# Zero-padded 128-row weights for RWKV's two low-rank products, and one buffer instead of three for its exponentials

## The chip, the cores and the metric

The kernel runs on one core of a Trainium2 chip. The metric is the time of one execution on the device in microseconds (us). The engines named below are PE (TensorE, matrix products), DVE (VectorE), ACT (ScalarE), POOL (GpSimd) and SP (SyncE, which here issues DMAs only). Each works through its own queue of instructions in order, and waits for the others by semaphores.

## The reference

One step of a single hybrid decoder layer: 1024 prompt tokens of a new sequence and 8 sample tokens that continue stored states, width 1024. A normalised input goes through one combined projection, whose columns feed three recurrences (RWKV-7, HGRN2, RG-LRU); their outputs go through an output projection, and then an MLP of width 4096 follows.

```python
xn = _rmsnorm(x, prm['norm1_g'][l])
P = (xn @ w_in).astype(F32)
pr, ph, pl = jnp.split(P, [RWKV_COLS, RWKV_COLS + HGRN_COLS], axis=-1)
pm = pr + prm['mu_shift'][l] * (pr_prev - pr)
...
mix = jnp.concatenate([o_r, o_h, o_l], axis=-1).astype(dt)
x = x + mix @ prm['w_out'][l]
xn2 = _rmsnorm(x, prm['norm2_g'][l])
x = x + jnp.square(jax.nn.relu(xn2 @ prm['mlp_w1'][l])) @ prm['mlp_w2'][l]
```

The change touches RWKV-7 alone. Of its columns `xw` and `xa` are 64 wide each; from them come the decay and the learning rate, by two low-rank products:

```python
r, k, v, xw, xa, xg = jnp.split(pm, [c, 2 * c, 3 * c, 3 * c + W_LORA, 3 * c + W_LORA + A_LORA], axis=-1)
w_log = -jax.nn.softplus(-(w0 + jnp.tanh(xw) @ w_up)) - 0.5
decay = jnp.exp(-jnp.exp(w_log))
a = jax.nn.sigmoid(a0 + xa @ a_up)
g = jax.nn.sigmoid(xg) @ g_up
...
S = S * wt[:, :, None, :] + sa[..., None] * (kkt * at)[:, :, None, :] + vt[..., None] * kt[:, :, None, :]
```

## The kernel before, in words

Channels lie on the 128 partitions and tokens along the free dimension. The large products (projections `in`, output projection `out`, MLP `up` and `dn`) take three passes each: weights and activations are split into a high and a low part (`wh`, `wl`, `xh`, `xl`, the type fp32r), and the kernel adds xh·wh, xl·wh and xh·wl (`dense_steps`). The small products of the recurrences are plain fp32, and one of them shows in the trace as two matmuls of the same shape. All products are recorded at one line (L74, the helper `mm`) and all transposes at L78, so that the trace tells them apart by the names of their tiles.

The program has two stages. Stage 1 projects and runs the recurrences; its tokens go in two halves of 512 (`hf` 0 and 1; the 8 sample tokens are with the second). RWKV's six heads are three blocks `j` of 128 channels, and each half has two quarters `qt` of 256 tokens, so that there are 12 parts `q` = (j, hf, qt). A part passes through `rw_operands` (operands from the projected columns), `rw_inverse` (the inverse within chunks of 64 tokens), `rw_chain` (four chunks after another with the state) and `rw_finish` (group norm, gate). Stage 2 is the MLP.

In stage 1 generators for all these are woven into one program (`weave`): each yields after a piece of work and names a delay or an event that it waits for, and the planner takes the next one that is due by its own estimate of PE time; the projections fill what is left. **PE's order is that of the code so written.** The order on DVE, ACT and POOL is set by the list scheduler behind the language, from priorities and modelled durations. So an edit can move instructions on those three queues far from the edited line, while PE's rows stay.

What the change touches:

- `waup` [128, 384] is one tile with two weights: rows 0 to 63 hold w_up, rows 64 to 127 a_up. The tile `xwa` (in the trace `pm_wa`) has tanh(xw) in rows 0 to 63 and xa in rows 64 to 127. The product `pw` (decay) uses rows 0 to 63 of both, `pa` (learning rate) rows 64 to 127; each is made once in a part, and each waits in ACT's tanh (L513, L522). `rw_sample_lora` makes the same products for the 8 sample tokens (`s_lora`).
- `ee` [128, 4, 65] is the exponential of the cumulated decay of a part, with a 1.0 ahead of each chunk (written by POOL's memset, L533). `ar` (two DVE operations, the first at L550) reads all of it. Later `rw_chain` reads the last column of each chunk as `wc`, to scale the state (POOL `ws` L691, DVE `st` L697). Thus it has three buffers.
- `hst` holds states of HGRN2 per chunk, in ten buffers.

Other names that the trace shows at these places: `t` is scratch of a part; `ir_kk` (L245 on DVE, then a power on POOL at L129) and `t` (L248), transposed by PE as `pb_kk`, form the norm of the key; `s_…` are the sample tokens' operands (L775 to L807); `ot` (L728) is the normalised output of a part, which PE transposes as `oT`; `gs` its group-norm sums; `rh` (L670) the right-hand side of a chunk, which PE multiplies into `ch`; `hf`, `lf`, `b` and `kq` belong to HGRN2 (L855 to L932); `xsq` is the square for the first norm.

Of the kernel before, what the change touches and what calls it, by code (L numbers as in the profile page):

```python
# [9 lines left out]
F32 = mybir.dt.float32  # L10
# [7 lines left out]
P = 128  # L18
# [9 lines left out]
QT = 256  # L28
NQ = QT // 64
C = 64  # L30
# [21 lines left out]
def kernel(ctx: ExitStack, tc: tile.TileContext, i, o):  # L52
# [169 lines left out]
    nsp2 = const.tile([P, 2], F32, name="nsp2")  # L222
    V.tensor_scalar(nsp2, sp2, -2.0, None, op0=ALU.mult)

    waup = const.tile([P, 384], F32, name="waup")
    gup = const.tile([P, 384], F32, name="gup")


# [262 lines left out]
    def rw_operands(q):  # L491

        j, hf, qt = PARTS[q]
        n = f"{j}_{hf}_{qt}"
        q0 = qt * QT
        qs = slice(q0, q0 + QT)
        jc = slice(j * P, (j + 1) * P)
        yield ("lora", hf)
        yield ("rkv", j, hf)
        xwa, _ = lora[hf]  # L500
        r, k, v = rkv[j, hf]

        def ck(ap):
            return ap.rearrange("p (c t) -> p c t", t=C)

        r_, k_, v_ = r[:, qs], k[:, qs], v[:, qs]
        t1, t2, t3, t4, t5 = (w2(f"t{u}", n, 1) for u in range(1, 6))

        act(t2, k_, AF.Square, scale=vec("kk", j))

        pw = ps("o", f"pw_{n}")
        mm(pw[:, 0:QT], waup[0:64, jc], xwa[0:64, qs])
        act(t1, pw[:, 0:QT], AF.Tanh, bias=hw0[:, j:j + 1], scale=0.5)  # L513
        V.tensor_scalar(t1, t1, -DECAY, -DECAY, op0=ALU.mult, op1=ALU.add)
        yield D4
        pn = yield from head_inv_root(t2, QT, f"kk{n}", "o", 1e-24, t4)
        V.scalar_tensor_tensor(t4, k_, vec("kk", j), pn, op0=ALU.mult, op1=ALU.mult)
        V.tensor_tensor_scan(t2, rmask_f, t1, 0.0, op0=ALU.mult, op1=ALU.add)
        yield D5
        pa = ps("o", f"pa_{n}")  # L520
        mm(pa[:, 0:QT], waup[64:128, jc], xwa[64:128, qs])
        act(t3, pa[:, 0:QT], AF.Tanh, bias=ha0[:, j:j + 1], scale=0.5)  # L522
        if q >= 3:
            yield ("C", q - 3)
        if q >= 1:
            yield ("sc", q - 1)
        yield D6
        ee = rwp.tile([P, NQ, C + 1], F32, tag="ee", name=f"ee_{n}", bufs=3)
        ar = rwp.tile([P, NQ, 2, C], F32, tag="ar", name=f"ar_{n}", bufs=3)
        kb = rwp.tile([P, NQ // 2, 4, C], F32, tag="kb", name=f"kb_{n}", bufs=1)  # L530
        kbt = rwp.tile([P, NQ, P], F32, tag="kbt", name=f"kbt_{n}", bufs=3)
        uv = rwp.tile([P, NQ, P], F32, tag="uv", name=f"uv_{n}", bufs=3)
        G.memset(ee[:, :, 0:1], 1.0)  # L533
        act(ee[:, :, 1:C + 1], ck(t2), AF.Exp)
        act(t1, t2, AF.Exp, scale=-1.0)

        pt = ps("o", f"vT_{n}")
        for c in range(NQ // 2):
            tr(pt[:, c * P:(c + 1) * P], v[:, q0 + c * P:q0 + (c + 1) * P], ident)
        pt4 = pt[:, 0:NQ // 2 * P].rearrange("p (c x) -> p c x", x=P)  # L540
        S.copy(uv[0:64, 0:NQ:2, :], pt4[0:64])
        S.copy(uv[64:128, 1:NQ:2, :], pt4[64:128])
        ck4 = "p (c x t) -> p c x t"
        V.scalar_tensor_tensor(t5, t3, 1.0, t4, op0=ALU.add, op1=ALU.mult)
        V.scalar_tensor_tensor(kb[:, :, 1:3, :], t5.rearrange(ck4, x=2, t=C), 0.5, t1.rearrange(ck4, x=2, t=C),
                               op0=ALU.mult, op1=ALU.mult)
        V.tensor_scalar(t3, t3, hka[:, j:j + 1], omka[:, j:j + 1], op0=ALU.mult, op1=ALU.add)
        V.tensor_tensor(t3, t3, k_, op=ALU.mult)
        V.tensor_tensor(kb[:, :, 0:4:3, :], t3.rearrange(ck4, x=2, t=C), t1.rearrange(ck4, x=2, t=C), op=ALU.mult)
        V.scalar_tensor_tensor(ar[:, :, 0, :], ck(t4), -1.0, ee[:, :, 0:C], op0=ALU.mult, op1=ALU.mult)  # L550
        V.tensor_tensor(ar[:, :, 1, :], ck(r_), ee[:, :, 1:C + 1], op=ALU.mult)
        ev(("A", q), L_OPS)
        V.scalar_tensor_tensor(t5, r_, vec("rk", j), t3, op0=ALU.mult, op1=ALU.mult)
        yield D7

        pt = ps("o", f"kbt_{n}")
        for c in range(NQ):
            src = kb[:, c // 2, 2 * (c % 2):2 * (c % 2) + 2, :].rearrange("p x t -> p (x t)")
            tr(pt[:, c * P:(c + 1) * P], src, ident)
        S.copy(kbt, pt.rearrange("p (c x) -> p c x", x=P))  # L560
        if q >= 2:
            yield ("P", q - 2)
        yield D8
        bo = w2("bo", n)
        pb = ps("o", f"bonus_{n}")[:, 0:QT]
        mm(pb, bones, t5)
        V.tensor_tensor(bo, pb, v_, op=ALU.mult)
        if qt == 1:
            free["pm"] += 3
        live[q] = dict(ee=ee, ar=ar, kb=kb, kbt=kbt, uv=uv, bo=bo)  # L570
        ev(("A2", q), L_EV)
        yield D9

# [78 lines left out]
    def rw_chain(q):  # L652
# [1 line left out]
        j, hf, qt = PARTS[q]  # L654
        n = f"{j}_{hf}_{qt}"
        yield ("B", q)
        ee, ar, kbt, uv, sc, ym, xm = (live[q][x] for x in ("ee", "ar", "kbt", "uv", "sc", "ym", "xm"))
        pt = ps("ch", f"ch_{n}")
        po = pt[:, QT:2 * QT]
        for c in range(NQ):  # L660
            st = rw_state[j]
            b = brow[c % 2]
            first = st is None
            mv = xm[b, (c // 2) * 2:(c // 2) * 2 + 2, :].rearrange("p h v -> p (h v)")
            if first:
                rh = mv
            else:
                mm(pt[b, 0:P], ar[:, c, 0, :], st)
                rht = rwp.tile([P, P], F32, tag="rh", name=f"rh{c}_{n}", bufs=1)
                V.tensor_tensor(rht[b, :], pt[b, 0:P], mv, op=ALU.add)  # L670
                rh = rht[b, :]
                yield D16
            for h in range(2):
                hc = slice(h * 64, h * 64 + 64)
                mm(pt[b, hc], ym[b, (c // 2) * 2 + h, :], rh[:, hc])
            V.tensor_copy(uv[b, c, :], pt[b, 0:P])
            yield D17
            for h in range(2):
                hp = slice(h * 64, h * 64 + 64)
                mm(pt[hp, P:P + 64], kbt[:, c, hp], uv[:, c, hp])  # L680
            out = po[krow[c % 2], (c // 2) * P:(c // 2) * P + P]
            if not first:
                mm(out, ar[:, c, 1, :], st, stop=False)
            for h in range(2):
                hp = slice(h * 64, h * 64 + 64)
                mm(out[:, hp], sc[:, 2 * c + h, 64:128], uv[:, c, hp], start=first, stop=first or h == 1)
            wc = ee[:, c, C:C + 1]
            sn = rw_st[j][c % 2]
            if not first:
                ws = rwp.tile([P, P], F32, tag="ws", name=f"ws{c}_{n}", bufs=2)  # L690
                G.tensor_scalar(ws, st, wc, 0.0, op0=ALU.mult, op1=ALU.add)  # L691
            for h in range(2):
                hp = slice(h * 64, h * 64 + 64)
                if first:
                    V.tensor_scalar(sn[hp, hp], pt[hp, P:P + 64], wc[hp], None, op0=ALU.mult)
                else:
                    V.scalar_tensor_tensor(sn[hp, hp], pt[hp, P:P + 64], wc[hp], ws[hp, hp], op0=ALU.mult, op1=ALU.add)  # L697
            rw_state[j] = sn
            if c == NQ - 1:

                if q >= 1:
                    yield ("N", q - 1)
                ot = w2("ot", n, 1)
                sums = small.tile([P, 2, NQ], F32, tag="gs", name=f"gs_{n}", bufs=2)
                for g in range(NQ):
                    act(ot[:, g * 64:(g + 1) * 64], po[:, g * 64:(g + 1) * 64], AF.Copy, accum_out=sums[:, 0, g:g + 1])
                live[q].update(ot=ot, sums=sums)
                ev(("C", q), 0.5)
            yield D18
# [33 lines left out]
    def rw_sample_lora():  # L743
        tcol = slice(HT, HW)
        xwa, sg = lora[1]
        out = hgp.tile([P, 3, 3, NB], F32, name="s_lora")
        for q, (w, x) in enumerate(((waup[0:64], xwa[0:64]), (waup[64:128], xwa[64:128]), (gup, sg))):
            pl = ps("h", f"s_lora{q}")
            for j in range(3):
                mm(pl[:, j * NB:(j + 1) * NB], w[:, j * P:(j + 1) * P], x[:, tcol])  # L750
# [151 lines left out]
    def hg_half(j, hf, lf, kin, q, iv, gs):  # L902
# [101 lines left out]
        for c in range(NCK):  # L1004
            st = hg_state[j]
            pc = ad[:, c % 2, (c // 2) * C:(c // 2 + 1) * C]
            sn = pool.tile([P, C], F32, tag="hst", name=f"hst{c}_{n}", bufs=10)
            if st is None:
                V.tensor_copy(sn, pc)
            else:  # L1010
# [271 lines left out]
    def projections():  # L1282
# [3 lines left out]
        for hf in range(2):  # L1286
            for group, j in ORDER[hf]:
                yield from dict(w=rw_lora, r=rw_proj, h=hg_proj, l=lru_proj)[group](j, hf)
                if (group, hf) == ("w", 0):
                    x_load(1, place=tc.keep_in_program_order)  # L1290
                    ev(("x", 1), 8.0)
                    for dst, name in ((cmask, "masks"), (waup, "waup"), (gup, "gup"), (cst, "lcst")):
                        nc.sync.dma_start(dst, i[name])
                    for h in range(2):
                        nc.sync.dma_start(lruw[h * 64:h * 64 + 64, :, h * 64:h * 64 + 64], i["lruw"][h])
            if hf == 0:
# [255 lines left out]
```

## Time and profile before

| | before |
|---|---|
| time, median of 3 runs (lowest, highest) | 1618.23 us (1614.12, 1618.76) |
| the profiled execution's own time | 1615.32 us |
| its span in the trace | 1613.5 us |
| granted PE clock, mean over the span | 0.967 |
| PE busy | 1534.4 us, 95% of the span, 12158 matmuls |
| DVE busy | 775.8 us, 48% |
| ACT busy | 637.1 us, 39% |
| POOL busy | 376.9 us, 23% |
| DMA, mean share of 16 queues' time: software queue, hardware queue | 26.3%, 15.3% |
| read from HBM | 144.12 MB |

"Busy" is the time in which an engine had an instruction in execution. PE's matmuls are pipelined, so their durations overlap: what a matmul costs PE is read from the distance between the starts of its neighbours, not from its own duration. "Granted clock" is the share of full speed at which PE was let run. In a list of instructions in order of time a row gives start, duration, engine, line, operation, tiles, shapes and a count; a bracket at its end gives how long the engine had stood idle before it, and what released it. In a table by stretches a row gives the stretch, its length, the busy time of PE, PE's weight loads, DVE, ACT and POOL with counts, then the granted clock, the share of DMA and the GB/s.

### The profile page before, as it was taken

The numbers are of one execution on the slowest core, as the hardware profiler recorded it, in microseconds if no ns is written. First come the engines' busy times: TensorE is split into PE (matmuls) and PEld (weight loads), VectorE is DVE, ScalarE is ACT, GpSimd is POOL, SyncE is SP. The second block draws the span as 40 slices with busy tenths as digits, with TensorE's granted clock in tenths as the row PEclk, the third lists the DMA queues.
The fourth block names the chain that finished last, engine by engine and source line by source line (L and its number), as shares of the span: only waits on it lengthen the run. The fifth ranks groups of instructions, "written<-read, shape, count | busy, mean of one in ns | idle before, by whom it ended". The sixth has DMA issues, their size and how long they took to land. (4 is left out here: it accounts for less than half of the span.)

```text
span 1613.5 us, 29358 instructions
## 1 busy us (share of the span) xinstructions
PE 1534.4 (95%) x12158; PEld 1310.5 (81%) x12158; DVE 775.8 (48%) x1765; ACT 637.1 (39%) x1361; POOL 376.9 (23%) x492
## 2 busy tenths in 40 slices
PE   8879899999899999899987999999999999999997
PEld 6657677688788788777787889989898989899887
DVE  7476656775656676675465222222232222222224
ACT  4444633653445355355344323233232423233232
POOL 4462312322323423423222010111101010111111
PEclk8979989999799999999999999999999999999999
DMA  6524424333243434434433353545445353544342
GB/s 216 134 53 95 90 67 92 80 80 86 60 91 75 100 80 101 99 81 113 113 119 103 82 109 80 108 85 104 83 101 92 79 110 81 104 85 89 58 90 106
DMA packets 54501, 152.18 MB, mean 94 GB/s; under 512 B 7104, under 2 KB 7392, under 8 KB 54368
## 3 DMA queue, kind: packets, MB, share of 16 engines
q0 software_dynamic: 24416, 70.67, 26.3%
q1 hardware_dynamic: 29808, 79.61, 15.3%
q8 instruction: 95, 1.56, 0.4%
q14 instruction: 38, 0.31, 0.1%
q10 hardware_dynamic: 144, 0.04, 0.0%
HBM read 144.12 MB, written 6.17 MB: 93 GB/s over the span
## 5 line engine op out<-in xcount | busy, mean ns | idle before, releaser
L74 PE MATMUL in<-xh,wl_in 128*128 128x512 f32 (+3 forms) x648 | 226.3, 349 | 6.5 <-DMA wl_in<-in_w_in 6.5
L74 PE MATMUL in<-xl,wh_in 128*128 128x512 f32 (+3 forms) x648 | 224.4, 346 | 3.4 <-DVE xl L357 3.4
L74 PE MATMUL in<-xh,wh_in 128*128 128x512 f32 (+3 forms) x648 | 225.4, 348 | 0.0
L74 PE MATMUL dn<-hh,wl_w 128*128 128x264 f32 (+2 forms) x696 | 223.3, 321 | 0.2 <-DMA wl_w<-in_w 0.2
L74 PE MATMUL dn<-hh,wh_w 128*128 128x264 f32 (+2 forms) x696 | 223.0, 320 | 0.0
L74 PE MATMUL dn<-hl,wh_w 128*128 128x264 f32 (+2 forms) x696 | 223.0, 320 | 0.0
L1440 DVE TENSOR_TENSOR mix<-mix,dn 128x512 f32<-128x512 f32 (+2 forms) x192 | 98.4, 512 | 241.6 <-PE dn L74 241.6
L268 POOL DMA_DIRECT2D wl_w<-in_w x88 | 76.3, 874 | 577.3 <-ACT hh L1370 323.6
L263 ACT ACTIVATE wh_w<-raw_w 128x512 fp32r<-128x512 f32 (+1 forms) x90 | 70.6, 784 | 272.5 <-PE dn L74 224.5
L1369 DVE SCALAR_TENSOR_TENSOR rl<-up,rl 128x512 f32<-128x512 f32 (+2 forms) x96 | 49.6, 516 | 222.3 <-ACT rl L1368 222.3
L74 PE MATMUL up<-nxh,wh_w 128*128 128x264 f32 (+1 forms) x512 | 145.7, 285 | 1.5 <-DVE rl L1369 1.3
L74 PEld LDWEIGHTS in<-xh,wl_in 128*128 128x128 f32 x648 | 128.2, 198 | 22.5 <-DMA wl_in<-in_w_in 8.0
L74 PE MATMUL up<-nxl,wh_w 128*128 128x264 f32 (+1 forms) x512 | 145.0, 283 | 0.5 <-POOL nxl L1268 0.5
L74 PE MATMUL up<-nxh,wl_w 128*128 128x264 f32 (+1 forms) x512 | 145.2, 284 | 0.0
L74 PEld LDWEIGHTS dn<-hh,wl_w 128*128 128x128 f32 x696 | 131.0, 188 | 13.8 <-DMA wl_w<-in_w 3.8
L74 PEld LDWEIGHTS in<-xl,wh_in 128*128 128x128 f32 x648 | 127.8, 197 | 17.5 <-DVE xl L357 4.3
L74 PEld LDWEIGHTS in<-xh,wh_in 128*128 128x128 f32 x648 | 128.6, 198 | 15.8 <-issue 4.7
L74 PEld LDWEIGHTS dn<-hl,wh_w 128*128 128x128 f32 x696 | 131.1, 188 | 10.0
L74 PEld LDWEIGHTS dn<-hh,wh_w 128*128 128x128 f32 x696 | 131.2, 188 | 9.2
L74 PE MATMUL up<-nh,wl_w 128*128 128x512 f32 x256 | 102.7, 401 | 5.9 <-DMA wl_w<-in_w 5.9
L1368 ACT ACTIVATE rl<-up 128x512 f32<-128x512 f32 (+2 forms) x96 | 43.3, 451 | 152.4 <-PE up L74 152.4
L74 PE MATMUL up<-nh,wh_w 128*128 128x512 f32 x256 | 102.6, 401 | 0.0
(438 smaller groups left out, 3215.8 us busy)
## 6 DMA issues: line engine op xcount, KB each, us to landing
raw_in<-in_w_in SPq DMA_DIRECT2D x53, 512.0 KB, 3.4
wl_in<-in_w_in POOLq DMA_DIRECT2D x49, 512.0 KB, 5.6
raw_w<-in_w SPq DMA_DIRECT2D x32, 512.0 KB, 3.3
raw_w<-in_w SPq DMA_DIRECT2D x64, 256.0 KB, 2.7
wl_w<-in_w POOLq DMA_DIRECT2D x30, 512.0 KB, 5.4
wl_w<-in_w POOLq DMA_DIRECT2D x58, 256.0 KB, 4.1
raw_out<-in_w_out SPq DMA_DIRECT2D x16, 512.0 KB, 3.4
wl_out<-in_w_out POOLq DMA_DIRECT2D x8, 512.0 KB, 5.6
```

What stands on the lines that cost most here:

```text
L74: PE.matmul(out, lhsT, rhs, start=start, stop=stop)
L263: act(wh[:, ks], raw[:, ks], AF.Copy)
L268: G.dma_start(wl[:, ks], src[:, ks], accum_op=ALU.add)
L1368: act(rl[:, :n], pt[:, :n], AF.Relu)
L1369: V.scalar_tensor_tensor(rl[:, :n], pt[:, :n], 0.0, rl[:, :n], op0=ALU.max, op1=ALU.mult)
L1440: V.tensor_tensor(x2[m][:, c0:c0 + n], x2[m][:, c0:c0 + n], pt[:, :n], op=ALU.add)
```

## The change

Two weight tiles of 128 rows take the place of `waup`: `wup` has w_up in rows 0 to 63 and zeros below, `aup` zeros above and a_up in rows 64 to 127. The products `pw`, `pa` and `s_lora` then run over all 128 rows of `xwa`; the zeros cancel the other half. `ee` keeps one buffer: its last columns are copied into a small tile `wc` [128, 4] with three buffers, which `rw_chain` reads instead. `hst` has nine buffers.

```diff
-    waup = const.tile([P, 384], F32, name="waup")
+    wup, aup = (const.tile([P, 384], F32, name=nm) for nm in ("wup", "aup"))
+    G.memset(wup[64:128], 0.0)
+    G.memset(aup[0:64], 0.0)
...
-        mm(pw[:, 0:QT], waup[0:64, jc], xwa[0:64, qs])
+        mm(pw[:, 0:QT], wup[:, jc], xwa[:, qs])
...
-        mm(pa[:, 0:QT], waup[64:128, jc], xwa[64:128, qs])
+        mm(pa[:, 0:QT], aup[:, jc], xwa[:, qs])
...
-        ee = rwp.tile([P, NQ, C + 1], F32, tag="ee", name=f"ee_{n}", bufs=3)
+        ee = rwp.tile([P, NQ, C + 1], F32, tag="ee", name=f"ee_{n}", bufs=1)
+        wc = rwp.tile([P, NQ], F32, tag="wc", name=f"wc_{n}", bufs=3)
...
         act(t1, t2, AF.Exp, scale=-1.0)
+        V.tensor_copy(wc, ee[:, :, C])
...
-            wc = ee[:, c, C:C + 1]
+            wc = wcs[:, c:c + 1]
...
-        for q, (w, x) in enumerate(((waup[0:64], xwa[0:64]), (waup[64:128], xwa[64:128]), (gup, sg))):
+        for q, (w, x) in enumerate(((wup, xwa), (aup, xwa), (gup, sg))):
...
-            sn = pool.tile([P, C], F32, tag="hst", name=f"hst{c}_{n}", bufs=10)
+            sn = pool.tile([P, C], F32, tag="hst", name=f"hst{c}_{n}", bufs=9)
...
-                    for dst, name in ((cmask, "masks"), (waup, "waup"), (gup, "gup"), (cst, "lcst")):
+                    for dst, name in ((cmask, "masks"), (gup, "gup"), (cst, "lcst")):
                         nc.sync.dma_start(dst, i[name])
+                    for h, w in enumerate((wup, aup)):
+                        hp = slice(h * 64, h * 64 + 64)
+                        nc.sync.dma_start(w[hp], i["waup"][hp])
```

On PE every row stands where it stood, with other weights in 24 + 6 products. SP has one load more, ahead of `lruw`. POOL has two memsets more at the start. DVE has 12 copies more, one in each part ahead of the first `ar`. Line numbers after the weight tiles are 3 to 8 higher in the changed kernel. Beyond that the scheduler has moved rows on DVE and POOL, and the following places are those that matter for what is said below.

The first is DVE's queue around 410 to 419 us, where the sixth part (j, hf, qt = 2, 0, 1) is in its chain (`rh`), the output of the fifth is normalised (`ot`), and the samples of RWKV's first block (`s_…`) and HGRN2's second half (`b`, `kq`) are prepared. Before, the four `ot` stood four rows above this piece:

```order
L910 SCALAR_TENSOR_TENSOR b_1_4680<-rmask,lf_1_4674 128x256 x2
L924 TENSOR_TENSOR kq_0_1_4693<-b_1_4680 128x512
L924 TENSOR_TENSOR kq_0_1_4802<-b_1_4680 128x512
L786 SCALAR_TENSOR_TENSOR s_kk_4159<-s_kk_4159,s_q_4160 128x8
L802 TENSOR_TENSOR s_tm_4149<-s_st_4148,s_kk_4159 128x512
L787 SCALAR_TENSOR_TENSOR s_ka_4162<-s_kk_4159,s_a_4153 128x8
L788 TENSOR_SCALAR s_q_4160<-s_a_4153,vt 128x8
L789 SCALAR_TENSOR_TENSOR s_kn_4161<-s_q_4160,sm_k 128x8
L790 SCALAR_TENSOR_TENSOR s_bo_4163<-sm_r,vt,s_kn_4161 128x8
L775 TENSOR_SCALAR s_a_5774<-s_a_5774 128x8
L670 TENSOR_TENSOR rh_2_0_1_4242<-ch_0_1_4240,xm_0_1_3492 64x128
```

The same place of the changed kernel on DVE:

```order
L791 SCALAR_TENSOR_TENSOR s_kk_4177<-s_kk_4177,s_q_4178 128x8
L807 TENSOR_TENSOR s_tm_4167<-s_st_4166,s_kk_4177 128x512
L792 SCALAR_TENSOR_TENSOR s_ka_4180<-s_kk_4177,s_a_4171 128x8
L793 TENSOR_SCALAR s_q_4178<-s_a_4171,vt 128x8
L675 TENSOR_TENSOR rh_2_0_1_4260<-ch_0_1_4258,xm_0_1_3508 64x128
L915 SCALAR_TENSOR_TENSOR b_1_4700<-rmask,lf_1_4694 128x256 x2
L794 SCALAR_TENSOR_TENSOR s_kn_4179<-s_q_4178,sm_k 128x8
L780 TENSOR_SCALAR s_a_5796<-s_a_5796 128x8
L733 TENSOR_SCALAR ot_0_0_4107<-ot_0_0_4107,gs_0_0_4108 128x64 x4
L929 TENSOR_TENSOR kq_0_1_4713<-b_1_4700 128x512
L929 TENSOR_TENSOR kq_0_1_4822<-b_1_4700 128x512
```

`rh` now stands ahead of `b` and both `kq`, and the four `ot` behind `rh` and `b`.

The second is POOL's queue at the same time (`gs` and `s_q` are the powers that the group norm and the samples wait for, `wl_in` the issue of a weight load). Before:

```order
L129 TENSOR_TENSOR gs_2_0_0_4092<-gs_2_0_0_4092,mhalf_64 128x4
L268 DMA wl_in2176_1_4187<-in_w_in 128x1024
L891 TENSOR_SCALAR hf0_1_3854<-hf0_1_3854,nfA_121,fA_112 128x520
L129 TENSOR_TENSOR s_q0_4160<-s_q0_4160,mhalf_64 128x8
L929 TENSOR_TENSOR kq0_0_1_4693<-kq0_0_1_4693,hf0_1_3854 128x256
L929 TENSOR_TENSOR kq1_0_1_4802<-kq1_0_1_4802,hf0_1_3854 128x128x2
L803 TENSOR_TENSOR s_st0_4148<-s_st0_4148,s_w0_4152 128x512
```

POOL there in the changed kernel:

```order
L129 TENSOR_TENSOR s_q0_4178<-s_q0_4178,mhalf_64 128x8
L896 TENSOR_SCALAR hf0_1_3870<-hf0_1_3870,nfA_121,fA_112 128x520
L129 TENSOR_TENSOR gs_2_0_0_4108<-gs_2_0_0_4108,mhalf_64 128x4
L271 DMA wl_in2176_1_4205<-in_w_in 128x1024
L808 TENSOR_TENSOR s_st0_4166<-s_st0_4166,s_w0_4170 128x512
L934 TENSOR_TENSOR kq0_0_1_4713<-kq0_0_1_4713,hf0_1_3870 128x256
L934 TENSOR_TENSOR kq1_0_1_4822<-kq1_0_1_4822,hf0_1_3870 128x128x2
```

The power of `s_q` now comes first and that of `gs` third, and `s_st` has gone ahead of the two `kq`.

The third is one of the places at which POOL sets the 1.0 of the next part's `ee`, here that of the seventh part. Before, it was the fifth row of this piece:

```order
L129 TENSOR_TENSOR ir_kk2_0_1_2990<-ir_kk2_0_1_2990,mhalf_64 128x4
L268 DMA wl_in1280_1_3089<-in_w_in 128x1024
L691 TENSOR_SCALAR ws3_1_0_1_3219<-st1_0_178,ee_1_0_1_1953 128x128
L583 COPY ym_0_1_0_4371<-cmask_88 128x256
L533 MEMSET ee_0_1_0_4127 128x4
L436 TENSOR_SCALAR pm_wa1_3086<-praw_wa1_3085,omm_94 128x520
```

The same piece of POOL's queue in the changed kernel:

```order
L129 TENSOR_TENSOR ir_kk2_0_1_3004<-ir_kk2_0_1_3004,mhalf_64 128x4
L537 MEMSET ee_0_1_0_4143 128x4
L271 DMA wl_in1280_1_3103<-in_w_in 128x1024
L696 TENSOR_SCALAR ws3_1_0_1_3235<-st1_0_181,wc_1_0_1_1964 128x128
L588 COPY ym_0_1_0_4389<-cmask_88 128x256
L439 TENSOR_SCALAR pm_wa1_3100<-praw_wa1_3099,omm_94 128x520
```

The memset now follows the power `ir_kk` of the part before (`2_0_1`), and with a single buffer it waits until DVE's `ar` of that part has read `ee`. It is moved in this way in all parts but the first.

More of the change, by code (lines that the diff above doesn't have):

```diff
@@ L569, in rw_operands @@
             free["pm"] += 3
-        live[q] = dict(ee=ee, ar=ar, kb=kb, kbt=kbt, uv=uv, bo=bo)
+        live[q] = dict(wcs=wc, ar=ar, kb=kb, kbt=kbt, uv=uv, bo=bo)
         ev(("A2", q), L_EV)
@@ L656, in rw_chain @@
         yield ("B", q)
-        ee, ar, kbt, uv, sc, ym, xm = (live[q][x] for x in ("ee", "ar", "kbt", "uv", "sc", "ym", "xm"))
+        wcs, ar, kbt, uv, sc, ym, xm = (live[q][x] for x in ("wcs", "ar", "kbt", "uv", "sc", "ym", "xm"))
         pt = ps("ch", f"ch_{n}")
```

## The prediction

> **What bounds the kernel now.** I read the page first, then the table by stretches for the two stages, then PE's instructions in order of time and their waits, and last DVE's and POOL's instructions around those waits.
>
> ```profile
> PE 1534.4 (95%) x12158; PEld 1310.5 (81%) x12158; DVE 775.8 (48%) x1765; ACT 637.1 (39%) x1361; POOL 376.9 (23%) x492
> ...
> 55.00:827.00 772.00, 723.74 (x7103) 582.93 (x7102) 508.42 (x1230) 363.18 (x877) 249.67 (x315) 0.95 0.39 89
> 827.00:1613.50 786.50, 766.22 (x4888) 692.06 (x4887) 232.02 (x457) 249.20 (x446) 98.85 (x119) 0.99 0.44 93
> ```
>
> PE is busy 95% of the span, and the next engine 48%. The change lies in the first of the two stretches, stage 1 after its start-up. There PE is busy 723.74 of 772.00 us, so 48 us are waits of PE; the rest is PE's own pace. The second stretch is the MLP, which it does not touch. So what can change is (a) how long PE takes for the 24 products, (b) PE's waits, which the moved rows on DVE and POOL may shorten or lengthen.
>
> **The change part by part.** First the products. Their own durations promise nothing:
>
> ```profile
> L74 PE MATMUL pw<-pm_wa,waup x24: 375/480/793, 55.7 to 652.0; 64*128 64x256 f32 x24
> L74 PE MATMUL gate<-pm_xg,gup x24: 377/379/483, 191.0 to 801.0; 128*128 128x256 f32 x24
> ```
>
> The shortest `pw` of 64 rows takes 375 ns, the shortest `gate` of 128 rows and the same width 377. (There are 12 `pw` products of two matmuls each; `pa` has the same count and shape.) But the starts of the neighbours tell another tale. Between full 128-row products, first a `pw`, then a `bonus` of 128 rows and the same width:
>
> ```profile
> 55.34 0.39 PE L74 MATMUL in<-xh,wh_in 128*128 128x512 f32 x1
> 55.66 0.70 PE L74 MATMUL pw<-pm_wa,waup 64*128 64x256 f32 x2
> ...
> 56.62 0.39 PE L74 MATMUL in<-xh,wl_in 128*128 128x512 f32 x1
> ...
> 78.09 0.39 PE L74 MATMUL in<-xl,wh_in 128*128 128x512 f32 x1
> 78.32 0.59 PE L74 MATMUL bonus<-t,bones 128*128 128x256 f32 x2
> ...
> 78.99 0.39 PE L74 MATMUL in<-xh,wh_in 128*128 128x512 f32 x1
> ```
>
> One `in` is left out in each piece. From the `in` ahead to the second `in` behind it is 56.62 − 55.34 = 1.28 us with `pw` and 78.99 − 78.09 = 0.90 with `bonus`: the product with 64 rows costs 0.38 us more, by a later start ahead of it and behind it. Where the neighbour ahead is itself of 64 rows (`ch`), only the edge behind is left:
>
> ```profile
> 496.62 0.70 PE L74 MATMUL pw<-pm_wa,waup 64*128 64x256 f32 x2
> 497.25 0.39 PE L74 MATMUL in<-xh,wh_in 128*128 128x256 f32 x1
> 497.48 0.28 PE L74 MATMUL in<-xl,wh_in 128*128 128x256 f32 x1
> ...
> 539.88 0.70 PE L74 MATMUL bonus<-t,bones 128*128 128x256 f32 x2
> 540.23 0.47 PE L74 MATMUL in<-xh,wl_in 128*128 128x264 f32 x1
> 540.54 0.29 PE L74 MATMUL in<-xh,wh_in 128*128 128x264 f32 x1
> ```
>
> That is 497.48 − 496.62 = 0.86 against 540.54 − 539.88 = 0.66, so 0.20, of which I take 0.19 (half of 0.38). I went through PE's order at the 24 products: 9 have full products on both sides, 9 on one side, and 6 stand between others of a tiled shape, where I take nothing. One of the 9 is lost, since PE waits for DVE shortly behind it:
>
> ```profile
> 101.18 1.22 PE L74 MATMUL pa<-pm_wa,waup 64*128 64x256 f32 x2
> ...
> 95.00:115.00 20.00, 16.57 (x78) 11.67 (x78) 19.87 (x28) 9.66 (x13) 16.01 (x20) 0.71 0.29 64
> ```
>
> DVE is busy 19.87 of those 20 us, and PE only 16.57. So the switches give 8 × 0.38 + 9 × 0.19 = **4.75 us** less. As bounds: 9 × 0.38 = 3.4 if a one-sided edge gives nothing, 18 × 0.38 = 6.8 if it gives as much as two. The samples' 12 matmuls I leave at nothing.
>
> The Trainium skill bears on this from both sides. "TensorEngine Tiling (Array Packing)", section Key Properties, says that changing the tiling mode drains TensorE; the starts above agree. "TensorE: Matmul & The Clock Gate", in its section on why this matters for your kernels, says that a single matmul of K=32 takes the time of one of K=128; the durations of 375 and 377 ns agree, and by that alone this term would be nothing.
>
> Second, the moved rows. The longest wait of PE at a place where rows have moved is this one:
>
> ```profile
> 408.18 0.43 PE L74 MATMUL s_kk<-s_q,bones 128*128 128x8 f32 x2
> ...
> 414.22 0.38 PE L78 MATMUL oT<-ident,ot 128*128 128x128 f32 x2
> 418.67 0.68 PE L74 MATMUL ch<-rh,ym 64*64 64x64 f32 x4 [4.07 <-DVE rh L670]
> ...
> 408.88 0.98 DVE L728 TENSOR_SCALAR ot<-ot,gs 128x64 f32<-128x64 f32 x4 [1.13 <-POOL gs L129]
> ...
> 412.01 1.27 DVE L910 TENSOR_TENSOR_SCAN b<-rmask,lf 128x256 f32<-128x256 f32 x2 [1.42 <-ACT lf L885]
> ...
> 414.53 0.16 DVE L786 SCALAR_TENSOR_TENSOR s_kk<-s_kk,s_q 128x8 f32<-128x8 f32 x1
> 414.72 1.30 DVE L802 TENSOR_TENSOR s_tm<-s_st,s_kk 128x512 f32<-128x512 f32 x1
> 415.95 0.79 DVE L787 SCALAR_TENSOR_TENSOR s_ka<-s_kk,s_a 128x8 f32<-128x8 f32 x1
> 416.66 1.08 DVE L788 TENSOR_SCALAR s_q<-s_a,vt 128x8 f32<-128x8 f32 x1
> ...
> 418.32 0.29 DVE L670 TENSOR_TENSOR rh<-ch,xm 64x128 f32<-64x128 f32 x1
> ...
> 411.65 1.96 POOL L129 TENSOR_TENSOR s_q<-s_q,mhalf 128x8 f32<-128x8 f32 x1
> ```
>
> `rh` stands behind the scan `b`, both `kq` and the samples' operations. In the new order it stands behind `s_kk`, `s_tm`, `s_ka` and `s_q` only. PE's product `s_kk` ends at 408.6, DVE copies it out as `s_q` (128x8, taken at the 0.16 of DVE's `s_kk`), POOL's power, now first of its rows here, takes 1.96: 410.7. The four DVE operations and `rh` at the durations above are 0.16 + 1.30 + 0.79 + 1.08 + 0.29 = 3.6, so `rh` ends at 414.3; with `s_ka` and `s_q` at 0.16 too, being as small as `s_kk`, at 412.8. But `ot` now stands behind `rh`, and PE's `oT` stands ahead of `ch`. Behind `rh` come `b` 1.27, two small ones at 0.16, and the `ot` 0.98, together 2.6: `ot` ends between 415.4 and 416.9, `oT` takes 0.38, and `ch` starts between 415.8 and 417.3 in place of 418.67. I take 2.0 of the possible 1.4 to 2.9, nearer to the durations as measured; what is late next is `ot`. Outer bounds: the whole 4.07 if `b` is not waited for, and a loss of 1 if ACT's `lf`, for which the scan now holds `ot` up, comes a microsecond or two later. **−2.0 us.**
>
> Third, the 12 copies `wc` of 128x4 on DVE. The nearest row:
>
> ```profile
> L245 DVE TENSOR_SCALAR ir_kk<-pc_kk x12: 151/163/164, 59.1 to 655.2; 128x4 f32<-128x4 f32 x12
> PE pb_kk L78 <- DVE t L248: 10.7, 3, 8.9
> ```
>
> At 0.16 us each, they lie beside PE's work, DVE being idle for half the time, save where PE waits for DVE. PE waits for it three times with the key's norm `t`, which in the new queue can stand behind a copy: 3 × 0.16 = **+0.5 us**; bounds 0 and 12 × 0.16 = 1.9. Without DVE's slack it would be the latter.
>
> Fourth, POOL's `ee` memset. Today it waits for the chain three parts back; this wait goes, and a shorter one for DVE's `ar` of the part before takes its place, earlier in the queue:
>
> ```profile
> POOL ee L533 <- DVE st L697: 16.5, 7, 4.2
> ...
> 170.70 0.42 DVE L550 SCALAR_TENSOR_TENSOR ar<-t,ee 128x256 f32<-128x256 f32 x1
> 171.32 0.92 POOL L268 DMA_DIRECT2D wl_in<-in_w_in  x1 [4.42 <-ACT wl_in L267]
> ```
>
> Queued behind the memset are the next `wl_in` issue, `ws` and `ym`, for which PE waits through the weights and the state. At the tightest of the 11 places `ar` ends at 170.70 + 0.42 = 171.12, and POOL's next row starts at 171.32 for a reason of its own: 0.2 us to spare, nothing lost. ACT's Exp into the single `ee` waits for the same `ar`, of a part earlier, and so costs nothing. Nor does the 16.5 us that POOL stood idle gain anything: POOL is busy 23%.
>
> Fifth, the start: two memsets of 64x384 on POOL and one load more on SP. They push POOL's `xsq`:
>
> ```profile
> 5.39 5.46 POOL L315 TENSOR_TENSOR xsq<-mix 128x512 f32<-128x512 f32 x4
> ...
> 12.91 0.68 DVE L321 TENSOR_TENSOR xsq<-xsq,xsq 128x512 f32<-128x512 f32 x1
> ```
>
> `xsq` ends at 10.85 and DVE first adds at 12.91, so 2.06 us cover them; the weights arrive long before their first use at 55.66. The ninth of `hst`'s buffers I put at nothing: the rows that it waits for stand on PE right behind those that wait today.
>
> The sum is −4.75 − 2.0 + 0.5 = **−6.25 us**. Against the profiled execution's 1615.32 that is 1609.1. That execution is 2.9 below the median of the runs; I take the difference from the median: 1618.23 − 6.25 = **1612.0 us**.
>
> **The rivals.**
>
> *Only the switches.* `b` waits for ACT's `lf` so long that `ot` and `oT` take up all of the gain at 418: 1618.23 − 4.75 + 0.5 = 1614.0. For it: `ot` was ready at about 409.9 and now comes at 415.4 at the earliest. Against: the working above.
>
> *Nothing arrives.* PE gains a few tenths at 24 places and waits as much longer for the next DMA or DVE result: 48 us of waits stand in stage 1. 1618. For it: the equal durations. Against: between the waits PE runs for tens of microseconds without one.
>
> *The clock as well.* Behind the wait the granted clock was low:
>
> ```profile
> 419.00:424.00 5.00, 5.00 (x23) 3.26 (x22) 1.37 (x4) 0.64 (x2) 0.00 (x0) 0.51 0.00 0
> 115.70 0.68 PE L74 MATMUL W<-xm,sc 64*64 64x64 f32 x16 [1.95 <-DVE xm L640]
> 116.00:120.00 4.00, 4.00 (x25) 3.26 (x22) 0.00 (x0) 0.96 (x2) 0.77 (x2) 0.58 0.86 139
> ```
>
> PE ran at 0.51 for the 5 us after 419. If the shorter wait leaves the clock up for the whole stretch of about 6.8 us, 6.8 × 0.5 = 3.4 us more are gained: 1608.6. Against: a wait of 1.95 us at 115.70 was followed by a clock of 0.58. The Trainium skill, "TensorE: Matmul & The Clock Gate", Part 1, has the clock fall after an idle window of about 3.4 us; by that rule a wait of 2 us would leave it up and this rival would hold, but the row at 115.70 speaks against the rule.
>
> *Slower.* The memset is held up behind `ir_kk`: if DVE's `ar` comes later than today wherever DVE is crowded, POOL's `wl_in` and `ws` stand behind it. With 1.2 us at each of 10 places that is 12 − 6.25 = 5.75 more: 1624.0. It decides from about 0.63 us a place, where it eats the gain. For it: the slack of 0.2 at the tightest place. Against: the same rows, in which the other engines' work ahead of `ar` does not change.
>
> **How the numbers follow.** My forecast 0.52, only the switches 0.20, nothing 0.13, the clock 0.06, slower 0.09. A measurement of this kernel tells about 0.3%, 4.9 us, from no change: faster is below 1613.4, slower above 1623.1. The forecast's own range, from −6.8 − 2.9 to −3.4 − 1.4 + 1.9, is 1608.5 to 1615.3; of it some 0.44 is faster and 0.08 the same. With 0.08 of the second rival and the clock's 0.06, faster is 0.58. Slower is 0.09 and 0.02 of "nothing", so 0.11; the same is what is left, 0.31. The range goes down to 1606.5, two below the clock's case, and up to 1618.5, so that "slower" and some of "nothing" are left out.
>
> **What would show it.** In the new profile: the distance of the `in` around the first `pw` 0.90 instead of 1.28; PE's wait ahead of `ch` near 417 of about 2 us, or split with one ahead of `oT`; no idle time of POOL of more than some tenths ahead of the `ee` memset; the MLP's stretch unchanged at 786.5. A new wait of PE over 2 us in stage 1, at a place that is not named here, would make the prediction wrong.

## The result, and the profile after

The changed kernel took 1604.88 us in the median of 4 runs (1601.68 to 1607.80), against 1617.32 us for the kernel before (4 runs, 1614.12 to 1618.76). The ratio is 0.9925 with a 95% interval of 0.9896 to 0.9955: faster by 12.4 us, between 7.3 and 16.8. The forecast was 6.25 us faster, and 1604.88 lies 1.6 us below the range. Two later comparisons, with 8 runs of it each, gave medians of 1607.43 and 1607.92 us, which lie inside the range, and ratios of 0.9946 (0.9925 to 0.9966) and 0.9949 (0.9930 to 0.9968), that is 8.7 and 8.2 us: the first four runs were a little lucky, but the gain is larger than forecast in all three. The profiled execution took 1607.80 us, 7.5 less than that of before.

The page of the changed kernel, its engines, and its table by stretches, cut where the same work begins and ends as in that of before (length, busy time of PE, its weight loads, DVE, ACT and POOL, then clock, DMA share, GB/s):

```profile
PE 1524.0 (95%) x12158; PEld 1306.1 (81%) x12158; DVE 775.4 (48%) x1777; ACT 637.9 (40%) x1361; POOL 380.9 (24%) x494
```

```profile
54.00:819.50 765.50, 717.22 (x7104) 582.47 (x7103) 508.54 (x1242) 363.63 (x877) 252.70 (x317) 0.95 0.39 90
819.50:1606.00 786.50, 765.32 (x4888) 691.13 (x4886) 231.52 (x456) 249.31 (x446) 98.61 (x118) 0.99 0.44 92
```

The MLP is unchanged at 786.5 us. Stage 1 is 6.5 us shorter and the start 1.0. PE's waits in stage 1 are still 48 us: all of the gain lies in PE's busy time, 723.7 to 717.2.

The instructions of the changed kernel on PE in order of time, around its first `pw`:

```profile
54.41 0.39 PE L74 MATMUL in<-xh,wh_in 128*128 128x512 f32 x1
54.65 0.59 PE L74 MATMUL pw<-pm_wa,wup 128*128 128x256 f32 x2
54.89 0.58 PE L74 MATMUL in<-xl,wh_in 128*128 128x512 f32 x1
55.31 0.39 PE L74 MATMUL in<-xh,wl_in 128*128 128x512 f32 x1
```

55.31 − 54.41 = 0.90 us, where it was 1.28. If the starts of PE's matmuls in both traces are laid side by side, the distances at the 24 products come to 5.0 us less (to 4.9 for a second pair of executions).

The place at which the longest wait stood, in the changed kernel, PE's rows first and then DVE's:

```profile
399.55 0.43 PE L74 MATMUL s_kk<-s_q,bones 128*128 128x8 f32 x2
...
408.05 0.69 PE L78 MATMUL oT<-ident,ot 128*128 128x128 f32 x2 [2.20 <-DVE ot L733]
408.67 0.69 PE L74 MATMUL ch<-rh,ym 64*64 64x64 f32 x4
```

```profile
404.30 0.30 DVE L675 TENSOR_TENSOR rh<-ch,xm 64x128 f32<-64x128 f32 x1 [0.75 <-ACT lf L890]
404.61 2.72 DVE L915 TENSOR_TENSOR_SCAN b<-rmask,lf 128x256 f32<-128x256 f32 x2
...
407.38 0.97 DVE L733 TENSOR_SCALAR ot<-ot,gs 128x64 f32<-128x64 f32 x4
```

`rh` now ends 4 us before it is needed, and `ot` comes last; the wait of 4.07 us ahead of `ch` has become one of 2.20 ahead of `oT`. From the start of PE's `s_kk` to that of `ch` it is 408.67 − 399.55 = 9.12 us, before 418.67 − 408.18 = 10.49: `ch` starts 1.4 us earlier (1.6 in four other traces with the single buffer). Behind it PE is at half speed as before, for 6.8 us (0.51 after 419 before, here 0.50 after 409), so the prediction's clock rival did not come at the place for which it was put:

```profile
409.00:414.00 5.00, 4.83 (x21) 2.90 (x20) 3.01 (x7) 2.31 (x7) 1.66 (x2) 0.50 0.00 0
```

Two waits are new or longer. The waits of the changed kernel by engine (us in total, times, longest), and of the kernel before for the second of them:

```profile
POOL ee L537 <- DVE ar L555: 20.1, 8, 5.5
...
PE in L74 <- DMA wl_in<-in_w_in: 9.2, 5, 4.8
```

```profile
PE in L74 <- DMA wl_in<-in_w_in: 6.5, 4, 4.1
```

POOL stands idle ahead of the `ee` memset for 20.1 us at 8 places, against 16.5 at 7 before. And PE waits for one weight load more, near 110 us: 2.1 us in this trace, 1.7 and 3.2 in two later ones; before, it did not wait there. A new wait of over 2 us at a place that isn't named was the prediction's own sign of being wrong, and it has come. But it is a loss, and the measured time is off the other way.

Last the clock. The stretch from `gate` on, which holds the same work of PE (90 matmuls), before and after:

```profile
190.00:217.50 27.50, 23.23 (x90) 15.70 (x89) 16.44 (x37) 14.73 (x22) 6.31 (x7) 0.69 0.18 39
```

```profile
186.30:208.60 22.30, 19.68 (x90) 12.89 (x90) 15.22 (x36) 14.90 (x22) 6.26 (x7) 0.77 0.21 48
```

This stretch alone is 5.2 us shorter, at a clock of 0.77 against 0.69. The stretch holds one `pw`, and its switch is worth 0.2. In the profiled executions PE ran at half speed for 17.1 us from 198.6 us on before, and for 10.2 from 190.2 after the change. Which part of the change shortened it is seen in the experiments below: not the 128 rows.

### The profile page after: what moved, and what is told of

It reads as the page before. It is cut to its first block, busy times and chain, and to the rows that moved or that the text cites. A ratio compares the mean times of both kernels' runs of the same rounds, so it can differ in the third digit from the quotient of the medians.

```text
span 1606.0 us, 29383 instructions
## 1 busy us (share of the span) xinstructions
PE 1524.0 (95%) x12158; PEld 1306.1 (81%) x12158; DVE 775.4 (48%) x1777; ACT 637.9 (40%) x1361; POOL 380.9 (24%) x494
```

## The experiments

Each run records its mean granted clock, so that span × (1 − clock) is what was lost to a low clock if PE is the bound. The means over the runs of this study (of the kernel before without the first four), with the error of the mean:

| kernel | runs | time, us | granted clock | span × (1 − clock), us |
|---|---|---|---|---|
| before | 79 | 1616.7 ± 0.4 | 0.9667 ± 0.0003 | 53.8 |
| single buffer alone | 12 | 1614.5 ± 1.6 | 0.9684 ± 0.0010 | 51.0 |
| the change with 64-row products | 24 | 1614.2 ± 1.0 | 0.9678 ± 0.0008 | 52.0 |
| the change | 20 | 1607.0 ± 0.7 | 0.9709 ± 0.0006 | 46.8 |
| the same with needless products, 64 rows | 12 | 1611.7 ± 0.9 | 0.9737 ± 0.0007 | 42.3 |
| the change with needless products | 12 | 1600.3 ± 0.8 | 0.9789 ± 0.0003 | 33.7 |

**Both kernels once more.** No edit.

> The kernel before, once more, for its times with the granted clock of each run beside them, and for a second profile. Theory 1 (the clock's half-speed stretches fall by chance, another way in each execution): times between 1614 and 1619, median near 1617, clock anywhere in 0.966 to 0.973, and the second profile has another length of half-speed stretch after 197 us than the 17.1 us of the first. Theory 2 (a property of the kernel): clock near 0.967 in all runs, and the 17.1 us stretch is there again.

> The changed kernel, once more. Theory 1 (chance): median near 1611, that is 1617 less the 6.25 of the forecast, and clocks that overlap with those of the kernel before. Theory 2 (the changed kernel is granted a higher clock): median near 1605 again, clock 0.970 to 0.975 in all runs, so about 0.005 above the kernel before, which is 8 us of the span.

Measured: the kernel before 1615.86 us (12 runs, 1611.43 to 1623.01), clocks from 0.963 to 0.970; the changed one 1607.43 (8 runs), clocks from 0.969 to 0.973. Neither theory holds as it was put. Times of one kernel spread over more than 10 us with its clock, so chance plays a part. But the means differ by 0.004, and the 17.1 us stretch was there again in the second profile of before, and the one of 10.2 us in the second of after (6.8 in a third).

**The change with 64-row products.** The order, the copies and the single buffer stay.

```diff
-        mm(pw[:, 0:QT], wup[:, jc], xwa[:, qs])
+        mm(pw[:, 0:QT], wup[0:64, jc], xwa[0:64, qs])
...
-        mm(pa[:, 0:QT], aup[:, jc], xwa[:, qs])
+        mm(pa[:, 0:QT], aup[64:128, jc], xwa[64:128, qs])
...
+        for q, (w, x) in enumerate(((wup[0:64], xwa[0:64]), (aup[64:128], xwa[64:128]), (gup, sg))):
```

> The changed kernel with its order, its copies and its single buffer, but the products pw, pa and s_lora over 64 rows as before (slices of the padded tiles). If the switches are worth 4.75 us as forecast and the clock is chance: 4.75 us slower than the changed kernel. If the 128 rows also raise the granted clock (theory 2a): 9 to 12 us slower than the changed kernel, with a mean clock near 0.967. If the moved rows raise the clock (theory 2b): about 5 us slower than the changed kernel with the same clock as that, and about 7 us faster than the kernel before.

> The changed kernel with 64-row products, once more and beside the changed kernel, since the first comparison (6.4 us, each side known to about 1 or 1.5 us) doesn't tell 4.75 from 7. By the sum of the switches: 4 to 5.5 us slower than the changed kernel. If the padding also raises the clock: 7 or more, with a mean clock lower by 0.002 or more.

> The changed kernel beside it. If the first measurement (12.4 us faster than before) was partly the chance of the clock, it is 6 to 9 us faster than before here, as in the second (9).

Measured: ratios to before 0.9986 (0.9963 to 1.0009) and 0.9986 (0.9964 to 1.0008), so 2.3 us faster than before, not clear of none. Over all runs the 128 rows are worth 1614.2 − 1607.0 = 7.2 us (± 1.2), with the clock up by 0.003; side by side it is 6.4 and 6.9 us. The order on PE, ACT and POOL is that of the changed kernel, and on DVE one pair of rows is exchanged, so the difference is that of the rows of the products. The switches account for 4.9 of it. The time lies between the expectations, above the 4.75 of the switches alone and below the 9 to 12 of 2a; the clock of 0.968 is the one that 2a has, by which the 128 rows raise it.

The stretch from `gate` on, with the same 90 matmuls, in the first trace of this kernel:

```profile
188.10:208.20 20.10, 17.31 (x90) 10.93 (x89) 15.43 (x36) 14.65 (x22) 6.26 (x7) 0.92 0.22 53
```

It takes 20.1 us at a clock of 0.92, with half speed for 3.4 us (3.4 in the second trace too), and so is 2.2 shorter than in the changed kernel. At this place, then, the 128 rows did not hold the clock up; what they bring must lie elsewhere.

**The single buffer alone.** The kernel before, with `ee` in one buffer and the copies `wc`.

```diff
-        ee = rwp.tile([P, NQ, C + 1], F32, tag="ee", name=f"ee_{n}", bufs=3)
+        ee = rwp.tile([P, NQ, C + 1], F32, tag="ee", name=f"ee_{n}", bufs=1)
+        wc = rwp.tile([P, NQ], F32, tag="wc", name=f"wc_{n}", bufs=3)
...
+        V.tensor_copy(wc, ee[:, :, C])
...
-            wc = ee[:, c, C:C + 1]
+            wc = wcs[:, c:c + 1]
```

> The kernel before with only the single buffer of ee and the copies wc; the weights stay one tile of 64 + 64 rows. Its rows on DVE and POOL stand nearly as in the changed kernel. Forecast by the terms: -2.0 + 0.5, so 1.5 us faster than the kernel before, with PE's wait ahead of ch near 417 about 2 us instead of 4.07. Theory 2a (the 128 rows raise the clock): the same 1.5. Theory 2b (the moved rows do): 7 us faster. Either way it should agree with the run of 64-row products on the padded tiles within 1 us, as the two differ in the start alone.

Measured: 0.9988 (0.9961 to 1.0015), 1.9 us faster, also not clear of none, and within 0.3 of the run above in the mean. On PE the place near 407 us (this kernel's rows):

```profile
406.81 0.68 PE L78 MATMUL oT<-ident,ot 128*128 128x128 f32 x2 [2.89 <-DVE ot L730]
407.43 0.44 PE L74 MATMUL ch<-rh,ym 64*64 64x64 f32 x4
```

The wait ahead of `ch` is gone, as forecast, and stands ahead of `oT`, longer than the 2 us expected. The stretch from `gate` on in this kernel:

```profile
187.60:207.60 20.00, 15.72 (x90) 10.28 (x89) 15.33 (x36) 14.60 (x22) 6.25 (x7) 1.00 0.24 54
```

At full clock it is 7.5 us shorter than before, by the moved rows alone. Yet the whole gains only some 2 us, and half speed comes in elsewhere: for 3.4 us near 607 and for 10.2 near 651, where the kernel before had none and 3.4. So the moved rows bring some 2 us and the weights the rest, and theory 2b, with its 7 us, falls. No run has the padding without the single buffer.

**The switch and the clock by themselves.** A kernel in which PE alone runs pieces of products with no waits.

```diff
+    def seg(name, rows, n, count):
+        bank = psum.tile([P, 512], F32, tag="seg", name=name, bufs=2)
+        for _ in range(count):
+            PE.matmul(bank[:, 0:n], w[0:rows], x[0:rows, 0:n], start=True, stop=True)
+        stream(70)
...
+    mixed("m128", 128, 20)
+    mixed("m64", 64, 20)
```

> Nothing of the layer is computed (the outputs are zeros): PE alone runs pieces of products with no waits. First 20 fp32 products of 128x256, each followed by four fp32r products of 128x512, over 128 rows and then over 64 rows: if the switch costs 0.38 us as the trace of before shows, the piece with 64 rows takes 20 x 0.38 = 7.6 us longer; if the durations alone count, the same time. Then pieces of one product over and over, with 256, 128, 96, 64, 48 and 32 columns, over 128 rows and over 64, each after some 15 us of full products. Theory A (the clock is granted by the work on the array, columns x rows): the clock falls to 0.5 in pieces with 64 rows that have twice the columns of the first piece with 128 rows at which it falls. Theory B (by columns alone): the same pieces fall for 64 and 128 rows. Theory C (by idle time alone): none falls, as PE waits nowhere.

The first two products of each mixed piece, and then pieces of one product over and over, in order of time (start, duration):

```profile
27.85 0.59 PE L93 MATMUL m<-x,w 128*128 128x256 f32 x2
...
29.21 0.59 PE L93 MATMUL m<-x,w 128*128 128x256 f32 x2
...
61.87 0.70 PE L93 MATMUL m<-x,w 64*128 64x256 f32 x2
...
63.62 0.70 PE L93 MATMUL m<-x,w 64*128 64x256 f32 x2
...
196.15 29.19 PE L87 MATMUL s<-x,w 128*128 128x128 f32 x260
241.15 29.30 PE L87 MATMUL s<-x,w 64*128 64x128 f32 x260
286.38 33.63 PE L87 MATMUL s<-x,w 128*128 128x96 f32 x300
335.85 58.73 PE L87 MATMUL s<-x,w 64*128 64x96 f32 x300
413.07 40.30 PE L87 MATMUL s<-x,w 128*128 128x64 f32 x360
469.28 71.76 PE L87 MATMUL s<-x,w 64*128 64x64 f32 x360
559.71 73.07 PE L87 MATMUL s<-x,w 128*128 128x48 f32 x360
```

A product of 128 rows and four `in`-like ones take 29.21 − 27.85 = 1.36 us, with 64 rows 63.62 − 61.87 = 1.75: the switch costs 0.39, as the trace of before had it. Without a switch 64 rows are no dearer (29.19 against 29.30). But at 96 and 64 columns the pieces of 64 rows take nearly twice the time of those of 128 rows, and at 48 columns the latter do so too. The table by stretches of this kernel says why:

```profile
342.00:394.00 52.00, 52.00 (x247) 52.00 (x245) 0.00 (x0) 0.00 (x0) 0.00 (x0) 0.50 0.00 1
420.00:450.00 30.00, 30.00 (x271) 30.00 (x270) 0.00 (x0) 0.00 (x0) 0.00 (x0) 1.00 0.00 1
475.00:540.00 65.00, 65.00 (x308) 65.00 (x307) 0.00 (x0) 0.00 (x0) 0.00 (x0) 0.50 0.00 1
```

PE is busy all the time in the three stretches (64 rows by 96 columns, 128 by 64, 64 by 64), and the granted clock is 0.50, 1.00 and 0.50. It falls between 64 and 48 columns with 128 rows, and between 128 and 96 with 64: at the same number of rows × columns. Theory A holds; idle time isn't needed, and columns alone don't decide.

**Do rows of zeros count?** The same pieces, with half of the rows of the weights zero as a third form.

```diff
+    wz = pool.tile([P, P], F32, name="wz")
+    G.memset(wz[0:64], 0.5)
+    G.memset(wz[64:128], 0.0)
...
+        seg(f"all{n}", w, 128, n, count)
+        seg(f"zero{n}", wz, 128, n, count)
+        seg(f"half{n}", w, 64, n, count)
```

> Nothing of the layer is computed (the outputs are zeros). The pieces of one product over and over once more, with 112, 96, 64 and 56 columns, each in three forms: 128 rows of weights that are not zero (all), 128 rows of which 64 hold zeros (zero), and 64 rows (half). If the rows that a product occupies count for the clock, whatever they hold: zero stays at full clock wherever all does, with 64 columns too, while half falls at 96 and 64. If zeros don't count: zero falls wherever half does, and the padding of the change can't have raised the clock.

The pieces with 96 and with 56 columns, in order of time:

```profile
177.11 33.63 PE L90 MATMUL all<-x,w 128*128 128x96 f32 x300
226.49 33.63 PE L90 MATMUL zero<-x,wz 128*128 128x96 f32 x300
275.96 58.78 PE L90 MATMUL half<-x,w 64*128 64x96 f32 x300
...
555.98 40.30 PE L90 MATMUL all<-x,w 128*128 128x56 f32 x360
612.08 40.30 PE L90 MATMUL zero<-x,wz 128*128 128x56 f32 x360
668.26 74.41 PE L90 MATMUL half<-x,w 64*128 64x56 f32 x360
```

`zero` keeps pace with `all` throughout, and `half` falls to half speed at 96 and below (with 112 columns it took 33.75 us and kept the clock). So rows of zeros count, and padding can hold the clock up.

Whether the same holds in the layer can be read from its eleven traces. The clock changes there in steps of 3.41 us only (half speed lasts 3.4, 6.8, 10.2, 13.7 or 17.1 us, save where the program ends). For each piece of that length I add up rows × columns of its matmuls, at the time that a column of 128 rows takes at full speed in the isolated kernels (30.38 us for 140 of 256 columns in fp32, 16.16 us for 70 of 512 in fp32r), as a share of the piece. Of 233 pieces with a share under 0.36, 229 are followed by half speed; of 4775 above 0.46, only 4; of the 143 between, 64. In the isolated kernels it is 178 of 178 under 0.36 and none of 270 above 0.46.

One place shows the 128 rows at work. In three traces with 64-row products (the second of the change with 64 rows, the single buffer alone, and the one with needless products below) a piece begins at the `pw` near 419 to 421 us; its share is 0.39, and PE then runs at half speed for 17.1 us. In the third trace of the changed kernel a piece begins at this `pw` as well; its share is 0.45, and the clock stays up behind it. In the other two traces of the changed kernel the pieces lie elsewhere against the work. So where half speed falls differs from one execution to the next, and only means over many runs price it.

**Work for PE while it waits.** The changed kernel with 16 needless products of 128x512 ahead of products for which PE waits.

```diff
+    def fill(bank, n):
+        for _ in range(n):
+            PE.matmul(bank, bones, cmask.rearrange("p a b -> p (a b)")[:, 0:512], start=True, stop=True)
...
+        fill(pb, {"kk0_0_1": 7}.get(name, 0))
...
+        fill(pt, {2: 2, 3: 1, 4: 2, 9: 2}.get(q, 0))
...
+                fill(pt, int((t, hf) == (1, 0)))
```

> The changed kernel with 16 products of 128x512 that nobody needs, put on PE where it waits anyway: 7 ahead of the pb_kk near 97 us, one ahead of each of the two lg near 190, and 7 ahead of the oT of the third, fourth, fifth and tenth part. If the half-speed clock behind those waits comes from too little work in them, the clock stays up: mean granted clock higher by 0.003 to 0.006 than the changed kernel's and 4 to 9 us faster than it. If the clock doesn't answer to that: 0 to 3 us slower than the changed kernel, with the same clock.

> The changed kernel with the 16 needless products beside it: again about 17 us faster than the kernel before (9 faster than the changed one), clock 0.978 to 0.980.

Measured: ratios to before 0.9894 (0.9874 to 0.9913) and 0.9915 (0.9888 to 0.9943), medians 1598.93 and 1602.02 us. It is faster than both kernels: 6.7 us less than the changed one in the mean, as expected (4 to 9), at a clock of 0.979, which is more than expected. From the first `pw` to the first `up`, PE is at half speed for 37.5 and 34.1 us in two traces, against 71.7, 68.3 and 51.2 in three of the changed kernel. The stretch with the two `lg` in the changed kernel, and in this one, which begins this work 0.6 us later:

```profile
189.40:199.40 10.00, 8.98 (x22) 4.88 (x22) 4.72 (x9) 7.81 (x13) 3.23 (x4) 0.54 0.34 67
```

```profile
190.00:200.00 10.00, 8.58 (x42) 5.17 (x43) 5.36 (x11) 8.30 (x14) 3.27 (x4) 1.00 0.33 61
```

The clock stays at 1.00 where it was 0.54. PE gets through 42 matmuls in these 10 us in place of 22, two of the needless products (four matmuls) among them. In the second trace one piece of 3.4 us at half speed is left here.

**The same with 64-row products.** The edit of the products as above, on this kernel.

> The changed kernel with the 16 needless products, and with 64-row products for pw, pa and s_lora. With most of the half-speed stretches gone, the two kernels differ by the switches and by what clock is still lost. If the switches are worth 4.75 us and the rest of the 7 us that the padding brought was clock: 4 to 6 us slower than the one with 128 rows and needless products. If the switches are worth all of it: 7 us or more, at the same clock.

Measured: 1611.62 us, ratio to before 0.9972 (0.9953 to 0.9991); 11.4 us (± 1.2) slower than with 128 rows, at a clock of 0.974 against 0.979. The time answers to neither expectation alone. In the two traces the distances at the 24 products differ by 4.6 us, if waits are taken out and half-speed time is counted at half; what remains goes with the clock, of which 8.6 us more are lost (42.3 − 33.7). On DVE a few rows stand in another order in this kernel, so some of it may be theirs.

## Why the prediction came out as it did

**What bounds the kernel**: right. PE's waits in stage 1 stayed at 48 us, and all of the gain is PE's busy time. That also says that the 2.0 us that the sum took from the waits did not arrive in their total.

**The products, −4.75 us**: right in mechanism and size as a price of the switches. At the places it is 4.6 to 5.0 us in every pair of traces, without waits and half-speed time, and 0.39 us a switch by itself. (By PE's rows next to them the 24 are 9, 8 and 7, not 9, 9 and 6; that is 0.19 less in the sum.) Both pages of the Trainium skill had their part right: the durations agree, as "TensorE: Matmul & The Clock Gate" has it in its section on why this matters for your kernels, and the starts agree with the drain at a change of mode that "TensorEngine Tiling (Array Packing)", Key Properties, states. But what I expected to be lost near 101 us to DVE was lost near 110 us to a weight load instead.

**The moved rows, −2.0 us**: right at its place, if too large; −1.4 to −1.6 measured, with `ot` late next as said. The two scans took 2.72 us in place of 1.27, and `rh` came earlier than reckoned.

**The copies, +0.5**: too small to be seen; DVE's busy time didn't grow. All of the moved rows and the copies come to 2 to 2.5 us by two kernels, forecast 1.5, and neither of the two is clear of none by itself.

**POOL's memset, 0**: wrong as to the wait, since POOL stands 20.1 us ahead of it, and not some tenths. I had taken the slack from the places of before, without the rows ahead of it having moved up too. It has cost nothing that the runs show: the kernels with the single buffer alone and with 64-row products have the wait as well, and aren't slower than before.

**The step that failed is the clock.** The prediction took it up only as a rival, for the one stretch behind 418 us, with a chance of 0.06, and put nothing of it into the sum. The granted clock rose from 0.9667 to 0.9709 in the mean, which is 53.8 − 46.8 = 7 us less lost; in the means some 2 of these come with the moved rows, and 5 (± 1.7) with the 128 rows. I had argued about the clock by waits alone, also where I weighed the rule of the Trainium skill, "TensorE: Matmul & The Clock Gate", Part 1 (an idle window of about 3.4 us): the row at 115.70 spoke against the rule, and I drew from it that shorter waits wouldn't help, not that something other than idle time decides. In these runs it is the work on the array, rows × columns in the time, and the padded rows count. Thus the change has a second effect that the sum lacked: its 24 products weigh double for the clock, which tells where small fp32 products keep a piece of 3.41 us near the limit, as at the `pw` near 420 us.

Does it add up? For the 128 rows: 4.9 of switches and 52.0 − 46.8 = 5.2 of clock, less the new wait of 1.7 to 3.2 us near 110, which is at most 0.2 in the traces of the change with 64 rows, make 7 to 8; measured are 7.2. Each of these figures is known to 1 or 2 us only, so the sum agrees but proves little. For the moved rows: 2.5 us at most, of which 53.8 − 52.0 = 1.8 to 2.8 can be clock alone, so that the 1.4 won near 418 seems to be given back elsewhere. Where, and how much of the lost clock counts at all in stretches in which DVE is the bound, isn't settled. Nor is what each of the 24 products does for the clock: beyond the one place near 420 us no trace shows it.

## What to carry to other kernels

Look at the granted clock by stretches before you price an edit on PE, and count rows × columns that PE streams in the stretch, not only its idle time: small products can keep an engine that is always busy at half speed. Where a product with few rows stands between full ones, zero rows took no longer here, saved the switch's 0.39 us and helped to hold the clock up. Where PE must wait, work that nobody needs can be worth more than none. And price the clock by means over many runs: half speed in one trace, even in two, can lie where the next kernel or execution does not have it.

## What the runs showed that I had not expected

The clock fell to 0.50 with PE busy without a gap. With a matmul every 0.11 us (40.30 us for 360) it kept 1.00 at 128 rows × 56 columns and fell at 48, and with 64 rows it kept it at 112 columns and fell at 96; rows of zero weights counted in full. Executions of one kernel spread with the clock, 1608 to 1629 us for 79 of the kernel before, so that four runs told 12.4 us where twenty told 9.7.
